# A hybrid decoder layer: products of the modulation rows in the first and in the second half of attention

## The chip, the cores and the metric

The kernel runs on one NeuronCore of a Trainium2 chip. A time is the microseconds (us) of the device from the start to the end of one execution; the runs of a kernel are compared by their median. A profile is one execution recorded by the hardware profiler. In profiles PE is TensorE's matmul, PEld its weight load, DVE the vector engine (VectorE), ACT ScalarE, POOL GpSimd, and SP the sequencer that issues most DMAs here.

## The reference

One decoder layer on x of 512 tokens by 2048, float32. What matters here is in three places:

```python
mod = silu(c) @ w_ada + b_ada                    # w_ada: 2048 x 12288
sh1, sc1, gt1, sh2, sc2, gt2 = split(mod, 6)     # six rows of 2048
h = rms_norm(x, g_pre_mix) * (1 + sc1) + sh1
proj = h @ w_in       # q, k/v of three branches, gates, RG-LRU branches
o_att = nsa_attention(...)   # 16 heads; compressed, selected and window branch
hr = rg_lru(causal_conv(xr)) # 8 channel blocks
mix = concat(rms_norm(o_att), rms_norm(gelu(yr) * hr)) @ w_out
x = x + gt1 * rms_norm(mix, g_post_mix)
h = rms_norm(x, g_pre_mlp) * (1 + sc2) + sh2
x = x + gt2 * rms_norm(square(relu(h @ w_ff1)) @ w_ff2, g_post_mlp)
```

The rows gt1, sh2 and sc2 (numbers 2, 3 and 4 in the kernel) are needed after attention: gt1 when the output projection is evacuated, sc2 and sh2 when the input of the MLP is formed. gt2 (number 5) is needed at the very end.

## The kernel before, in words

A matrix product in float32 is made of three matmuls in a rounded type (`mm3`, L176): every operand is split into a rounded part by ScalarE (L102 for weights) and a rest by VectorE (L103). Weights come by DMAs of 512 KB on the SP queue into two raw tiles (`wr`, L84).

Stages in order: the modulation rows 0 and 1 and the first projections; attention of head groups 0 and 1 (`attention(0, n1)`, L996), a changeover that forms keys and values of groups 2 and 3 (L997 to L1000), attention of groups 2 and 3 (`attention(1, ...)`, L1001); then the output projection (L1018 to L1186) and the MLP. Below, the two calls are the first and the second half of attention.

A half has 64 units, one for each head, branch (selected, window) and chunk of 128 queries. A unit has scores on TensorE, a masked minimum with the branch's key count on VectorE (`soft1`, L736), an exponential on ScalarE (L738), a reciprocal and a product with the gate on VectorE (L746, L747), a scaling on ScalarE (L748), transposes on TensorE (L755), and the split of the transposed rows on both (L766, L767). `sm` is a small tile of a unit's statistics, in a ring of six. The loop of `attention` (L958) has 70 steps, each working on several units at different points of this chain. Between them `fill` takes pieces of other work from a list: projections of later heads and the RG-LRU branch.

A modulation row that is not needed early is computed as products on VectorE (`qdot`, L208). Row s is cut into 64 pieces (16 blocks of 128 outputs, 4 stretches of 512 inputs). A piece loads a tile `md` of 128x512 of `w_ada` by a DMA on SP (256 KB, L217), multiplies it by the same stretch of silu(c), which stands in a tile `ca` on all partitions, and sums along the row (L218: one three-operand instruction and the read of its accumulator). `md` has four buffers in attention; `ca` has one and is loaded anew (L216) after every 16 pieces. Each step of the loop adds MRATE = 0.8 to a counter, and as often as it holds a whole one a piece is issued: rows 2, then 4, then 3. Whatever of rows 3 and 4 is left goes into the output projection (`cdots`, L1121), evenly over 36 places. The 64 pieces of row 5 run in the MLP.

The order on each engine is not the order of this code. A scheduler orders the instructions of all engines by priority (the place in the code) and by when they can run according to its own model; each engine then runs its list strictly in that order. A piece depends only on a free `md` buffer, its load and `ca`, so the scheduler can place it ahead of its place in the code.

Of the kernel before, what the change touches and what calls it, by code (L numbers as in the profile page):

```python
# [7 lines left out]
F32 = mybir.dt.float32  # L8
F32R = mybir.dt.float32r
AF = mybir.ActivationFunctionType  # L10
OP = mybir.AluOpType
# [16 lines left out]
Q_REST, K_REST, XR_T, YR_T = 0, 6, 8, 16  # L28


NA1, NA2, NMS, NTMP, NXI, NPC, NSB, TD, MRATE, NMD, NRT = 4, 10, 22, 6, 4, 2, 11, 3, 0.8, 4, 6
JOIN = [2, 1, 1, 1] * 5 + [2, 1, 1, 0, 3]
HALF, CA_ = 512, 1
PX = 0
# [96 lines left out]
def hybrid_block_kernel(ctx: ExitStack, tc: tile.TileContext, xT, c, vec, wada, wst, win, wv0, wv1,  # L131
                        w1, w2, pe, wrg, wout, wff1, wff2, xN, out):
    nc = tc.nc
    V, A, T, G = nc.vector, nc.scalar, nc.tensor, nc.gpsimd
# [68 lines left out]
    QD = {s_: [(k, q_) for q_ in range(4) for k in range(KT)] for s_ in (2, 3, 4, 5)}  # L203
    dq = {s_: const.tile([128, 4, KT], F32, name=f"dq{s_}") for s_ in QD}
    CA = {}
    cad = dram.tile([1, D], F32, name="cad")

    def qdot(pool, s_, n, ring=("md", NMD)):  # L208
        for _ in range(min(n, len(QD[s_]))):
            k, q_ = QD[s_].pop(0)  # L210
            w = pool.tile([128, S], F32, name="md", tag=ring[0], bufs=ring[1])
            if k == 0 or CA["pool"] is not pool:
                CA["pool"] = pool
                ca = CA[0] = pool.tile([128, S], F32, name="ca", tag="ca", bufs=1)
                row = cad[0, S * q_:S * q_ + S]
                nc.sync.dma_start(ca, bass.AP(tensor=row.tensor, offset=row.offset, ap=[[0, 128], [1, S]]))  # L216
            nc.sync.dma_start(w, wada[s_, k, :, S * q_:S * q_ + S])  # L217
            (V.scalar_tensor_tensor(w, w, 0.5, CA[0], op0=OP.mult, op1=OP.mult,  # L218
                                                            accum_out=dq[s_][:, q_, k:k + 1]))

    def qvec(o, s_, base=None, plus=0.0):
# [35 lines left out]
    def fill(n):  # L257
        for _ in range(n):
            if stream:
                stream.pop(0)()  # L260
# [389 lines left out]
    bp = bst.enter_context(tc.tile_pool(name="bp", bufs=1))  # L650
# [21 lines left out]
    def quad(pair, ep):  # L672
        return [((2 * pair + i % 2), 2 * ep + i // 2) for i in range(4)]
# [24 lines left out]
    def cmp_a2(pair, ep):  # L698
        p_, d_ = PC[pair, ep]
        pf = p_.rearrange("p c e n -> p (c e) n")  # L700
        V.reduce_sum(d_, pf, axis=AX.X)
        V.reciprocal(d_, d_)
        for i, (g, e_) in enumerate(quad(pair, ep)):
            dv = d_.rearrange("p (c e) -> p c e", c=4)[:, :, i]
            V.tensor_mul(dv, dv, gates[:, :, 3 * (4 * g + e_)])
        V.tensor_mul(pf, pf, d_[:, :, None].to_broadcast([128, 16, 32]))
# [12 lines left out]
    UN, HB = {}, {}  # L719

    def scores(u):
        h, br, ch = u
        n = 128 * (ch + 1)
        sp_ = ps("S")
        q_ = Q[h][:, 128 * ch:128 * ch + 128]
        T.matmul(sp_[:, :n], q_, KD[h // 4][:, br, 0, :n], start=True, stop=False)
        T.matmul(sp_[:, :n], q_, KD[h // 4][:, br, 1, :n], start=False, stop=True)
        UN[u] = [sp_]

    def soft1(u):  # L730
        h, br, ch = u
        n = 128 * (ch + 1)
        sp_ = UN[u][0]
        p_ = bp.tile([128, S], F32, name="pp", tag="pp", bufs=TD + 1)
        sm = bp.tile([128, 4], F32, name="sm", tag="sm", bufs=6)
        V.tensor_tensor_reduce(p_[:, :n], sp_[:, :n], mask[:, S - n:], scale=-0.125, scalar=3e38,  # L736
                               op0=OP.add, op1=OP.min, accum_out=sm[:, 0:1])
        A.activation(p_[:, :n], p_[:, :n], AF.Exp, bias=sm[:, 0:1], scale=-1.0, accum_out=sm[:, 1:2])  # L738
        UN[u] = [p_, sm]

    def soft2(u):
        h, br, ch = u
        n = 128 * (ch + 1)
        p_, sm = UN[u]
        gi = h * 3 + 1 + br
        V.reciprocal(sm[:, 2:3], sm[:, 1:2])  # L746
        V.tensor_mul(sm[:, 3:4], sm[:, 2:3], gates[:, ch, gi:gi + 1])  # L747
        A.activation(p_[:, :n], p_[:, :n], AF.Copy, scale=sm[:, 3:4])  # L748

    def trans(u):  # L750
        h, br, ch = u
        p_ = UN[u][0]
        pt = ps("T")
        for j in range(ch + 1):
            T.transpose(pt[:, 128 * j:128 * j + 128], p_[:, 128 * j:128 * j + 128], ident)  # L755
        UN[u] = [pt]

    def evac_t(u):
        h, br, ch = u
        n = 128 * (ch + 1)  # L760
        if ch == 0:
            HB[h, br] = [bp.tile([128, 13, 128], F32R, name=n_, bufs=1) for n_ in ("pth", "ptl")]
        th, tl = HB[h, br]
        pv_ = UN.pop(u)[0][:, :n].rearrange("p (j q) -> p j q", q=128)
        sl = slice(ch, 3 * ch + ch + 1, 3)
        A.activation(th[:, sl], pv_, AF.Copy)  # L766
        V.tensor_sub(tl[:, sl], pv_, f(th[:, sl]))  # L767
# [174 lines left out]
        add(lambda k=k: pre_out(k))  # L942
    n3 = len(stream)

    nmod = [0.0]

    def attention(pair, natoms):
        seq, info = [], {}
        for ep in range(2):
            for i, (g, e_) in enumerate(quad(pair, ep)):  # L950
                for br in range(2):
                    for ch in range(4):
                        u = (4 * g + e_, br, ch)
                        info[u] = (ep, i, 4 * pair + e_)
                        seq.append(u)
        n = len(seq)
        goal, done = len(stream) - natoms, 0
        for s_ in range(-1, n + TD + 2):  # L958
            def get(k):
                return seq[k] if 0 <= k < n else None  # L960
            if get(s_ - 1):
                soft2(get(s_ - 1))
            if get(s_ - TD - 1):
                evac_t(get(s_ - TD - 1))
            if get(s_):
                soft1(get(s_))
            if 0 <= s_ < n and s_ % 32 == CA_:
                cmp_a(pair, s_ // 32)
            if get(s_ + 1):
                scores(get(s_ + 1))  # L970
            tot = natoms * (s_ + 2) // (n + TD + 3)
            k = tot - done
            fill(k // 2)
            if get(s_ - TD):
                trans(get(s_ - TD))
            fill(k - k // 2)
            done = tot
            if 0 <= s_ < n:
                if s_ % 32 == CA_ + 1:
                    cmp_a2(pair, s_ // 32)  # L980
                if s_ % 32 == CA_ + 2:
                    cmp_b(pair, s_ // 32)
            u = get(s_ - TD - 1)
            if u and u[2] == 3:
                ep, i, t = info[u]
                pv(u[0], u[1], i, PC[pair, ep])
                if u[1] == 1:
                    head_out(u[0], i, t)
            nmod[0] += MRATE
            while nmod[0] >= 1:  # L990
                qdot(bp, 2 if QD[2] else 4 if QD[4] else 3, 1)
                nmod[0] -= 1
        fill(natoms - done)

# [196 lines left out]
    for g in range(4):  # L1191
        for q in range(NA1):
# [3 lines left out]
            for r in range(4):  # L1196
                half, j = r // 2, 2 * g + r % 2
# [350 lines left out]
    for s, (kind, q, g) in enumerate(GR):  # L1548
        if kind == "f":
            k, n = q  # L1550
# [110 lines left out]
    for n_, key in enumerate(XTODO):  # L1661
        n, j, half = key
        for c_ in range(2):
            y = Y[key][:, 256 * c_:256 * c_ + 256]
            V.scalar_tensor_tensor(y, y, rs[:, 2 * j + c_:2 * j + c_ + 1], XT[key][:, 256 * c_:256 * c_ + 256],
                                   op0=OP.mult, op1=OP.add)
# [68 lines left out]
```

## Time and profile before

| | |
|---|---|
| median of 3 runs | 2198.32 us (2195.87 to 2200.69) |
| profiled execution, whole | 2199.99 us |
| its span, first to last instruction | 2198.3 us |
| mean granted TensorE clock | 0.982 |
| busy: TensorE, VectorE, ScalarE | 2093.1, 1879.1, 1392.2 us |
| pieces (L218) | 256 |

How to read it: the busy share is of an engine's time between the start and the end of its instructions; matmuls overlap, so TensorE can look busier than it is. An idle stretch in front of an instruction is put down to what ended it. The granted clock is 1.0 at TensorE's 2.4 GHz and 0.5 at 1.2 GHz.

### The profile page before, as it was taken

How to read it: one execution, taken by the hardware profiler on the slowest of the kernel's cores; microseconds unless marked ns; L12 is line 12 of the kernel's file. 1: busy time of each engine (PE TensorE's matmuls, PEld its weight loads, DVE VectorE, ACT ScalarE, POOL GpSimd, SP SyncE). 2: the span in 40 equal slices, each digit the busy share in tenths (PEclk: the TensorE clock that was granted, in tenths of full speed). 3: DMA queues.
4: the chain of work that ended last, by engine and by line, in shares of the span. 5: the costliest groups of instructions: out<-in, count | busy, mean ns of one | idle time of the engine just before them, and what ended most of it. 6: DMA issues, size and time to landing. Idle time of an engine off the chain costs nothing.

```text
span 2198.3 us, 39410 instructions
## 1 busy us (share of the span) xinstructions
PE 2093.1 (95%) x14621; PEld 1911.7 (87%) x14621; DVE 1879.1 (85%) x3764; ACT 1392.2 (63%) x2536; POOL 63.5 (3%) x119
## 2 busy tenths in 40 slices
PE   7998999989999989999999999998999999999995
PEld 3686777778877867899999999998999999999995
DVE  8987989877887677889999999999888887887788
ACT  4349879648995226765555555545766777767764
POOL 0000000000000000000000000000000000000010
PEclk9999999999999999999999999999999999999998
DMA  9764544762127886555555555566766544544453
GB/s 380 309 234 139 189 158 149 219 199 68 59 85 225 275 290 203 180 191 175 184 180 171 175 186 178 194 206 207 248 218 217 188 164 141 165 151 157 138 171 116
DMA packets 138818, 411.12 MB, mean 187 GB/s; under 512 B 18225, under 2 KB 25281, under 8 KB 134273
## 3 DMA queue, kind: packets, MB, share of 16 engines
q1 hardware_dynamic: 126178, 341.49, 46.6%
q0 software_dynamic: 12448, 67.12, 8.8%
q8 instruction: 115, 1.88, 0.4%
q14 instruction: 77, 0.63, 0.1%
HBM read 366.58 MB, written 41.97 MB: 186 GB/s over the span
## 4 chain that ended last, share of the span: by engine, by line
PE 52%; issue 26%; DVE 12%; ACT 5%; DMA 5%; POOL 0%; SPq 0%; DVEq 0%; POOLq 0%; ACTq 0%
PE ps_pj L1132 3%; PE ps_pj L1133 3%; PE ps_pj L1134 3%; DMA md<-wada 3%; DVE fl L1300 3%; PE ps_pj L1479 2%; PE ps_pj L1480 2%; PE ps_pj L1481 2%; PE ps_T L1132 2%; PE ps_T L1134 2%; PE ps_T L1133 2%; PE ps_S L1134 2%; PE ps_S L1132 2%; PE ps_S L1133 2%; PE ps_S L1479 2%
## 5 line engine op out<-in xcount | busy, mean ns | idle before, releaser
L1299 ACT ACTIVATE fh<-fs 128x1024 fp32r<-128x1024 f32 x256 | 272.9, 1066 | 324.7 <-DVE fs L1318 139.6
L1300 DVE TENSOR_TENSOR fl<-fs,fh 128x1024 fp32r<-128x1024 f32 x256 | 312.3, 1220 | 98.2 <-ACT fh L1299 95.7
L1299 ACT ACTIVATE fh<-fr 128x768 fp32r<-128x768 f32 (+2 forms) x296 | 217.1, 735 | 67.5 <-PE ps_pj L1133 13.3
L1300 DVE TENSOR_TENSOR fl<-fr,fh 128x768 fp32r<-128x768 f32 (+2 forms) x296 | 239.9, 814 | 11.3 <-ACT fh L1299 11.3
L102 ACT ACTIVATE sl<-wr 128x512 fp32r<-128x512 f32 (+2 forms) x252 | 145.6, 606 | 150.7 <-DMA wr<-wout 93.4
L218 DVE SCALAR_TENSOR_TENSOR md<-md,ca 128x512 f32<-128x512 f32 x256 | 171.4, 685 | 62.8 <-DMA md<-wada 39.7
L103 DVE TENSOR_TENSOR sl<-wr,sl 128x512 fp32r<-128x512 f32 (+2 forms) x252 | 163.6, 662 | 47.8 <-ACT sl L102 32.7
L1315 DVE TENSOR_TENSOR fs<-fr 128x512 f32<-128x512 f32 x256 | 175.2, 684 | 5.8 <-DMA fr<-wff 4.1
L1479 PE MATMUL ps_pj<-fh,AH 128*128 128x256 f32 x602 | 169.1, 281 | 1.1 <-ACT ps_pj L1459 1.0
L1480 PE MATMUL ps_pj<-fl,AH 128*128 128x256 f32 x602 | 169.1, 281 | 0.0
L1481 PE MATMUL ps_pj<-fh,AL 128*128 128x256 f32 x602 | 168.8, 281 | 0.0
L177 PE MATMUL ps_pj<-AH,sl 128*128 128x512 f32 x384 | 161.7, 421 | 0.1
L179 PE MATMUL ps_pj<-AH,sl 128*128 128x512 f32 x384 | 153.1, 399 | 0.7 <-DVE sl L103 0.7
L178 PE MATMUL ps_pj<-AL,sl 128*128 128x512 f32 x384 | 153.2, 399 | 0.0
L1479 PEld LDWEIGHTS ps_pj<-fh,AH 128*128 128x128 f32 x602 | 113.9, 189 | 2.1 <-ACT ps_pj L1459 2.1
L1480 PEld LDWEIGHTS ps_pj<-fl,AH 128*128 128x128 f32 x602 | 114.0, 189 | 0.4 <-DVE fl L1300 0.4
L1481 PEld LDWEIGHTS ps_pj<-fh,AL 128*128 128x128 f32 x602 | 114.0, 189 | 0.0
L1480 PE MATMUL ps_S<-fl,AH 128*128 128x256 f32 x394 | 110.4, 280 | 2.8 <-DVE fl L1300 2.8
L1479 PE MATMUL ps_S<-fh,AH 128*128 128x256 f32 x394 | 110.5, 280 | 1.3 <-ACT ps_S L1459 1.2
L1318 DVE TENSOR_TENSOR fs<-fs,fr 128x256 f32<-128x256 f32 x256 | 107.6, 420 | 3.5
L1481 PE MATMUL ps_T<-fh,AL 128*128 128x256 f32 x396 | 110.6, 279 | 0.0
L1479 PE MATMUL ps_T<-fh,AH 128*128 128x256 f32 x396 | 110.6, 279 | 0.0
(633 smaller groups left out, 7283.8 us busy)
## 6 DMA issues: line engine op xcount, KB each, us to landing
fr<-wff SPq DMA_DIRECT2D x276, 512.0 KB, 3.7
md<-wada SPq DMA_DIRECT2D x256, 256.0 KB, 4.3
uf<-ud POOLq DMA_DIRECT2D x32, 896.0 KB, 4.9
wr<-win SPq DMA_DIRECT2D x48, 512.0 KB, 3.7
ada<-wada SPq DMA_DIRECT2D x22, 1024.0 KB, 10.2
wr<-wout SPq DMA_DIRECT2D x36, 512.0 KB, 4.9
ud<-uf POOLq DMA_DIRECT2D x18, 896.0 KB, 5.2
ud<-uf POOLq DMA_DIRECT2D x14, 768.0 KB, 4.9
```

The lines of the kernel that those rows point to most:

```text
L103: self.nc.vector.tensor_sub(lo, raw, self.f(hi))
L177: T.matmul(o, wh, mh, start=start, stop=False)
L218: (V.scalar_tensor_tensor(w, w, 0.5, CA[0], op0=OP.mult, op1=OP.mult, accum_out=dq[s_][:, q_, k:k + 1]))
L1132: T.matmul(o, wh, b[0], start=start, stop=False, skip_group_check=True)
L1133: T.matmul(o, wh, b[1], start=False, stop=False, skip_group_check=True)
L1134: T.matmul(o, wl, b[0], start=False, stop=stop, skip_group_check=True)
L1299: A.activation(hi, src, AF.Copy)
L1300: V.tensor_sub(lo, src, f(hi))
L1315: V.tensor_add(v2(Sm[:, :512]), v2(R[:, 256:768]), R[:, None, :256].to_broadcast([128, 2, 256]))
L1479: T.matmul(o, uh, hi, start=first and k < 4 and t_ == 0, stop=False, skip_group_check=True)
L1480: T.matmul(o, uh, lo, start=False, stop=False, skip_group_check=True)
L1481: T.matmul(o, ul, hi, start=False, stop=last, skip_group_check=True)
```

## The change

The rate of pieces becomes 0.4 per step in the first half and 1.7 in the second. In the second half every fourth piece (while the step has a unit) no longer takes its factor 0.5 as a constant but from a fifth column of the unit's `sm`, which a memset fills with 0.5 just before. So this piece can't be placed ahead of the tile `sm` of its step.

```diff
-NA1, ..., TD, MRATE, NMD, NRT = 4, 10, 22, 6, 4, 2, 11, 3, 0.8, 4, 6
+NA1, ..., TD, MR, NMD, NRT = 4, 10, 22, 6, 4, 2, 11, 3, (0.4, 1.7), 4, 6
...
-    def qdot(pool, s_, n, ring=("md", NMD)):
+    def qdot(pool, s_, n, ring=("md", NMD), half=0.5):
...
-            (V.scalar_tensor_tensor(w, w, 0.5, CA[0], op0=OP.mult, op1=OP.mult,
+            (V.scalar_tensor_tensor(w, w, half, CA[0], op0=OP.mult, op1=OP.mult,
...
-        sm = bp.tile([128, 4], F32, name="sm", tag="sm", bufs=6)
+        sm = bp.tile([128, 5], F32, name="sm", tag="sm", bufs=6)
...
-    nmod = [0.0]
+    nmod, ndot = [0.0], [0]
...
-            nmod[0] += MRATE
+            nmod[0] += MR[pair]
             while nmod[0] >= 1:
-                qdot(bp, 2 if QD[2] else 4 if QD[4] else 3, 1)
+                half = 0.5
+                if pair and get(s_) and ndot[0] % 4 == 0:
+                    half = UN[get(s_)][1][:, 4:5]
+                    V.memset(half, 0.5)
+                qdot(bp, 2 if QD[2] else 4 if QD[4] else 3, 1, half=half)
+                ndot[0] += 1
                 nmod[0] -= 1
```

On VectorE in the second half, at its eighth and ninth unit, this stood before (pp and sm are a unit's probabilities and statistics, sl a weight's rest):

```order
L736 ISA pp_4921,sm_4922<-ps_S_4895,mask_1075 128x512
L736 ISA sm_4922 128x1
L767 TENSOR_TENSOR ptl_4833<-ps_T_4905,pth_4832 128x4x128
L746 RECIPROCAL sm_4922<-sm_4922 128x1
L747 TENSOR_TENSOR sm_4922<-sm_4922,gates_72 128x1
L736 ISA pp_4957,sm_4958<-ps_S_4925,mask_1075 128x128
L736 ISA sm_4958 128x1
L103 TENSOR_TENSOR sl_5070<-wr_4853,sl_5069 128x512
L746 RECIPROCAL sm_4958<-sm_4958 128x1
L747 TENSOR_TENSOR sm_4958<-sm_4958,gates_72 128x1
```

And at the same two units this stands now (md and ca are a piece's operands, dq2 its result, L994 the memset):

```order
L736 ISA pp_4859,sm_4860<-ps_S_4829,mask_1075 128x512
L736 ISA sm_4860 128x1
L736 ISA pp_4898,sm_4899<-ps_S_4863,mask_1075 128x128
L736 ISA sm_4899 128x1
L994 MEMSET sm_4932 128x1
L218 SCALAR_TENSOR_TENSOR md_4995,dq2_91<-md_4995,ca_4679 128x512
L746 RECIPROCAL sm_4860<-sm_4860 128x1
L218 SCALAR_TENSOR_TENSOR md_4966,dq2_91<-md_4966,sm_4932,ca_4679 128x512
L747 TENSOR_TENSOR sm_4860<-sm_4860,gates_72 128x1
L746 RECIPROCAL sm_4899<-sm_4899 128x1
L218 SCALAR_TENSOR_TENSOR md_4998,dq2_91<-md_4998,ca_4679 128x512
L747 TENSOR_TENSOR sm_4899<-sm_4899,gates_72 128x1
```

Three pieces, one of them tied to a unit's `sm`, have come between the unit's own instructions. Counted over the whole list, before the first, up to the 32nd, from the 32nd to the 64th, and between the 64th and the 65th mask-add (L736) stood 33, 39 and 40 pieces, and none between the 65th and the last; 80 after it, without row 5's. Now it is 33, 8, 0, 95, and 56 after the last.

On the SP queue this stood before from the end of the changeover into the second half (wr is a weight's raw tile):

```order
L217 DMA md<-wada 128x512 x6
L84 DMA wr<-win 128x1024
L217 DMA md<-wada 128x512 x3
...
L84 DMA wr<-win 128x1024 x3
L84 DMA wr<-wrg 128x256
L84 DMA wr<-win 128x1024 x2
...
L84 DMA wr<-win 128x1024 x6
```

And this stands now in the second half:

```order
L217 DMA md<-wada 128x512 x7
L84 DMA wr<-win 128x1024
L217 DMA md<-wada 128x512 x5
...
L217 DMA md<-wada 128x512 x4
L216 DMA ca<-cad 128x512
L217 DMA md<-wada 128x512
...
L84 DMA wr<-wrg 128x256
L217 DMA md<-wada 128x512 x3
```

The weight loads of the second half, which followed one another, now have the loads of pieces and of `ca` between them; in the changeover it is the other way round.

## Rows read from the trace of the kernel before

**Rows 1.** Page: span, and busy time, share and instructions of each engine

```profile
span 2198.3 us, 39410 instructions
...
PE 2093.1 (95%) x14621; PEld 1911.7 (87%) x14621; DVE 1879.1 (85%) x3764; ACT 1392.2 (63%) x2536; POOL 63.5 (3%) x119
```

**Rows 2.** Busy time by stretch; columns in the first line

```profile
core 0: us, PE busy (x) PEld busy (x) DVE busy (x) ACT busy (x) POOL busy (x), PEclk, DMA share, GB/s
215.00:314.00 99.00, 95.04 (x485) 77.24 (x485) 91.99 (x300) 84.11 (x202) 1.78 (x3) 1.00 0.55 177
314.00:417.00 103.00, 97.67 (x499) 78.25 (x498) 96.54 (x317) 82.79 (x195) 2.16 (x4) 1.00 0.55 168
417.00:482.00 65.00, 59.84 (x369) 52.72 (x367) 47.63 (x126) 26.22 (x53) 0.54 (x1) 0.98 0.73 239
482.00:653.00 171.00, 165.43 (x851) 134.74 (x851) 141.38 (x444) 153.01 (x362) 3.24 (x6) 0.99 0.21 66
653.00:700.00 47.00, 44.15 (x186) 34.62 (x187) 39.14 (x69) 29.19 (x56) 1.08 (x2) 0.89 0.66 207
700.00:840.00 140.00, 130.69 (x542) 102.21 (x541) 96.33 (x240) 40.84 (x89) 0.00 (x0) 0.96 0.83 276
...
340.00:380.00 40.00, 39.33 (x199) 31.52 (x198) 39.44 (x124) 38.44 (x91) 1.08 (x2) 1.00 0.48 152
```

**Rows 3.** Line L736 within 482 to 653: count, ns min/median/max, first and last start

```profile
L736 DVE CUSTOM_DVE_ANT_0 pp<-ps_S,mask x64: 266/477/692, 482.3 to 651.9; 128x128 f32<-128x128 f32 x16, 128x256 f32<-128x256 f32 x16, 128x384 f32<-128x384 f32 x16, 128x512 f32<-128x512 f32 x16
```

**Rows 4.** Busy time of L218 by stretch; two records make a piece

```profile
core 0: us, DVE busy (x), PEclk, DMA share, GB/s
215.00:314.00 99.00, 22.51 (x66) 1.00 0.55 177
314.00:417.00 103.00, 26.43 (x78) 1.00 0.55 168
417.00:482.00 65.00, 26.78 (x80) 0.98 0.73 239
482.00:653.00 171.00, 0.00 (x0) 0.99 0.21 66
653.00:700.00 47.00, 0.00 (x0) 0.89 0.66 207
700.00:840.00 140.00, 52.84 (x160) 0.96 0.83 276
```

**Rows 5.** Timeline of VectorE: start us, duration us, instruction

```profile
439.93 0.67 DVE L218 SCALAR_TENSOR_TENSOR md<-md,ca 128x512 f32<-128x512 f32 x1
440.54 0.07 DVE L218 DVE_READ_ACCUMULATOR md<-md,ca 128x1 f32 x1
440.54 0.68 DVE L218 SCALAR_TENSOR_TENSOR md<-md,ca 128x512 f32<-128x512 f32 x1
...
441.15 0.68 DVE L218 SCALAR_TENSOR_TENSOR md<-md,ca 128x512 f32<-128x512 f32 x1
```

**Rows 6.** Instructions of VectorE by line, 200 to 440: busy us, mean ns | idle before

```profile
L218 DVE SCALAR_TENSOR_TENSOR md<-md,ca 128x512 f32<-128x512 f32 x87 | 58.5, 681 | 12.4 <-DMA md<-wada 5.8 <-DMA ca<-cad 4.5 <-issue 2.1
...
L805 DVE SCALAR_TENSOR_TENSOR xc<-xp,vecs,xc 128x512 f32<-128x512 f32 x12 | 9.0, 746 | 0.0
...
L800 DVE MEMSET xp<- 128x3 f32 x5 | 0.3, 61 | 0.0
```

**Rows 7.** What L218 waited for within 215 to 482: us, times

```profile
  DMA md<-wada: 13.3, 12
  DMA ca<-cad: 8.7, 3
```

**Rows 8.** Changeover: waits (us, times, longest), and timeline rows of ScalarE and TensorE

```profile
ACT sl L102 <- DMA wr<-win: 14.7, 5, 5.3
...
475.15 0.63 ACT L102 ACTIVATE sl<-wr 128x512 fp32r<-128x512 f32 x1 [5.27 <-DMA wr<-win]
...
481.13 1.24 PE L685 MATMUL ps_pj<-kc,qd 128*128 128x64 f32 x5 [3.95 <-DVE qd L253]
```

**Rows 9.** Projection: timeline rows of SP, ScalarE and TensorE

```profile
802.89 0.33 SPq L216 DMA_DIRECT2D ca<-cad  x1
803.27 1.39 SPq L217 DMA_DIRECT2D md<-wada  x2
804.76 0.38 SPq L84 DMA_DIRECT2D wr<-wout  x1
...
811.48 1.15 ACT L102 ACTIVATE sl<-wr 128x512 fp32r<-128x512 f32 x2 [6.89 <-DMA wr<-wout]
...
807.08 0.39 PE L917 MATMUL ps_pj<-sl,AL 128*128 128x512 f32 x1
812.16 0.80 PE L915 MATMUL ps_pj<-sl,AH 128*128 128x512 f32 x1 [4.69 <-ACT sl L102]
...
817.72 0.80 PE L916 MATMUL ps_pj<-sl,AH 128*128 128x512 f32 x1 [3.18 <-DVE sl L103]
```

More of the change, by code (lines that the diff above doesn't have):

```diff
@@ L28 @@
 Q_REST, K_REST, XR_T, YR_T = 0, 6, 8, 16
-NA1, NA2, NMS, NTMP, NXI, NPC, NSB, TD, MRATE, NMD, NRT = 4, 10, 22, 6, 4, 2, 11, 3, 0.8, 4, 6
+NA1, NA2, NMS, NTMP, NXI, NPC, NSB, TD, MR, NMD, NRT = 4, 10, 22, 6, 4, 2, 11, 3, (0.4, 1.7), 4, 6
 JOIN = [2, 1, 1, 1] * 5 + [2, 1, 1, 0, 3]
```

## Prediction

> **What bounds the kernel now.** The page comes first: over the whole span TensorE is busy 95% and the Vector engine 85% [rows 1]. That is an average over stages, so the second view is the table of stretches, cut where the change cuts [rows 2]. 215 to 314 and 314 to 417 us hold the 32 + 32 softmax units of the first half of attention. 417 to 482 is the changeover, 482 to 653 the 64 units of the second half (its first and last mask-add start at 482.3 and 651.9 [rows 3]); then come its tail with the start of the output projection, and the projection up to 840.
>
> In that table the Vector engine is the busiest but for TensorE in the first half (92.0 of 99 us, 96.5 of 103) and has room in the second (141.4 of 171). TensorE's busy time overlaps itself and says little. ScalarE is busy 84 and 83 us in the two early stretches and 153 of 171, that is 89%, in the second half.
>
> The third view is the same table for line L218 alone, the pieces of the modulation rows, each with its accumulator read, so two records a piece [rows 4]. There are 33 pieces before 314, 39 up to 417, 40 in the changeover, none from 482 to 700, and 80 in the projection. So 112 were written for attention, 56 a half, yet all were done before the second half began: the scheduler had pulled them forward. This is what the reader should see: the half that the change loads has no piece at all now, and 29.6 us of idle Vector time.
>
> **The change part by part.**
>
> *Counts.* 70 steps at 0.4 give 28 pieces, at 1.7 some 118 (the last fraction is lost), 146 in all against 112. The rest of the 192 pieces of rows 2, 4 and 3 falls from 80 to 46. In the order on VectorE the counts are 33, 8, 0, 95, 10 and 46 where they were 33, 39, 40, 0, 0 and 80. A piece that is tied to a step keeps one of the four buffers, so at most a few loose ones can get ahead: the hold works.
>
> *Cost of one piece.* Three pieces in a row start 0.61 us apart, though each is shown with 0.68 us and a read of 0.07 [rows 5]: an instruction overlaps the end of the one before. I take 0.61 us. The 27 tied ones add a one-column fill of 0.061 us [rows 6]. Their factor is a column in place of a constant: a three-operand instruction with a column takes 0.746 us against 0.681 with a constant [rows 6], so 0.065 us more. Together 27 x 0.126 = 3.4 us.
>
> *Second half, 482 to 653: loss.* The Vector engine has 141.4 us of work there; 95 x 0.61 = 58.0 and 3.4 make 202.8 in 171. Since it works in order, 31.8 us is the least that this stretch grows, with no idle time left at all. The other end adds waits at the head of its queue. The vector ca is reloaded every 16 pieces into one buffer, and pieces waited 8.7 us in 3 reloads and 13.3 us for their own rows among 112 [rows 7]: six reloads at 2.9 and 95 pieces at 0.12 are 28.8 us, so 60.6 in all. The nearest rows are the early stretches, where this engine is the bound with pieces among the units: 92.9% and 93.7% busy [rows 2], and 98.6% in their densest part, 340 to 380 [rows 2]. I take 95%, since ScalarE would then be busy only 153 of 213: 202.8 / 0.95 = 213.5, a loss of 42.5 us.
>
> *Tail, 653 to 700: loss.* 10 pieces of 0.61 are 6.1 us beside 39.1 of 47 busy [rows 2]. They fit the 7.9 us of idle time, but stand ahead of the normalization that TensorE needs next: between 0 and 6.1, taken as 2.
>
> *First half from 314 on: gain.* 31 pieces leave, 18.9 us of Vector work, the most that can be won; the least is nothing, if TensorE (97.7 of 103 busy) is the real limit. Without them Vector has 77.6 us and ScalarE's 82.8 is the largest next to TensorE. At the 89% that ScalarE reaches in the second half this stretch would take 92.5, a gain of 10.5. I take 8, nearer to the TensorE row.
>
> *Changeover: gain.* All 40 pieces leave. Vector was no bound here (47.6 of 65 busy), so their own 24 us are worth nothing. But their loads share the SP queue with the weights: ScalarE waited 14.7 us for weights, 5.27 of it at 475, and TensorE then stood 3.95 us [rows 8]. TensorE's idle time here is 5.2 us and the lower clock (0.98) accounts for 1.3 [rows 2]: between 0 and 6.5, taken as 4.
>
> *Projection, 700 to 840: gain.* The same pattern. At 802.9 the reload of ca and two rows are issued ahead of a weight, ScalarE waits 6.89 us for it, TensorE stands 4.69 and then 3.18 us at 812 and 817 [rows 9], and the granted clock over the stretch is 0.96, where it was 1.00 from 215 to 417 [rows 2]. Its idle time is 9.3 us, the clock at most 4% of 140 = 5.6: between 0 and 14.9. 34 of 80 pieces leave; that share of 14.9 is 6.3, and I take 7.
>
> *Sum.* 42.5 + 2 - 8 - 4 - 7 = +25.5 us. The profiled execution took 2199.99 us, 1.7 us around its span; 2225.5. It lies 1.7 us above the median of the runs, 2198.32, so about 2224 is forecast.
>
> **The rivals.**
>
> *The relief outweighs the load (faster).* Where Vector bounds the first half, what leaves it shortens the time one to one, and the freed SP queue lets TensorE run without standing. With every relieved stretch at its end, 18.9 + 6.5 + 14.9 = 40.3, and the second half at its floor of 31.8 with the tail free, the kernel would take 2199.99 - 8.5 - 1.7 = 2190. It decides from the point where the second half grows by less than the relief gives. For it: Vector at 94% in the first half. Against it: the floor is a count that nothing shortens, and TensorE is already close to continuous in the relieved stretches. The Trainium skill (Perfetto Trace Analysis, Optimization Strategy) says that where the most-contended engine changes between regimes, interleaving them may help. That rule speaks for this rival. The trace agrees that the bound changes (Vector 94% in the first half, ScalarE 89% in the second), but the second half has 29.6 us of idle Vector time for 61.4 us of new work, so evening out turns into overloading.
>
> *Weights of the second half come late (slower still).* In the new order on SP four to seven loads of pieces stand between two weight loads of the second half, where weights stood alone. A row cannot be issued until the piece four or so before it has run, and the weight behind it waits. The measured price is 14.7 us of weight wait for 40 pieces in the changeover [rows 8], of which TensorE lost 5.2; at 95 pieces 12 us, and with a fall of the clock as at 812 (a matmul there takes 0.80 us instead of 0.39 [rows 9]) up to 20: 2236 to 2244. For it: the same pattern stalls the projection. Against it: TensorE has slack once Vector bounds the half, and DMA is busy only 21% there against 83% in the projection [rows 2]. The skill (DMA: Bandwidth & Descriptors, Anatomy of one DMA) states that a semaphore wait is held by the issuing sequencer before dispatch, the DMA engines do not wait. That is the blocking meant here, and the issue times around 802.9 agree.
>
> *The hold fails* and the pieces run ahead as before: then only 34 pieces would move out of the projection, between 2184 and 2200. The order excludes it, and I give it 1%.
>
> **How the numbers follow.** This kernel's measurements can tell about 0.2%, 4.4 us, from no change. Forecast (Vector bounds the second half, relief gives back less than half): 68%, own range 2208 to 2238, from the floor with middling relief up to 52 us of loss with the relief as taken. Late weights: 17%. Relief about equal to the load or above it: 14%, spread from 2190 to 2207; the failing hold: 1%. Of these 15, 8 are faster by over 0.2% (below 2193.9) and 7 within 0.2%, with 1 more from the forecast's low end. Slower: 84%. The range is 2203 to 2246: it leaves one in ten at the low end and one in ten above, where the second half's waits reach their upper end with little relief.
>
> **What would show it.** In the profile after, the 64 units of the second half should span about 212 us instead of 170 with the Vector engine busy over 93% and ScalarE down to some 72%; 95 pieces lie in that stretch. The 32 units before should take about 95 us instead of 103, and the changeover about 61. In the projection TensorE's idle time should fall from 9.3 to a few us. I am wrong in the main step if the second half grows by under 32 us (then a piece costs less than 0.61 us beside other work), wrong in its size if Vector is idle over 10% there, and wrong in the relief if the stretch from 314 shortens by over 15 us or not at all.

## The result and the profile after

The changed kernel takes 2226.12 us (median of 4 runs, 2222.99 to 2229.05) where the kernel before takes 2197.46 beside it: a ratio of 1.0124, 95% interval 1.0109 to 1.014 (estimated from the single runs; the quotient of the two medians is 1.0130). Slower was forecast, at 2224 us. The profiled execution took 2224.39 us, 24.4 more than that of before.

The page of the changed kernel, its span and busy times, against [rows 1]:

```profile
span 2222.7 us, 39427 instructions
...
PE 2106.4 (95%) x14621; PEld 1922.0 (86%) x14621; DVE 1876.8 (84%) x3791; ACT 1398.9 (63%) x2538; POOL 63.7 (3%) x119
```

The Vector engine has done the same work (1876.8 us, 1879.1 before): nothing is added but 27 small fills, the time comes from the place. The table of stretches, cut at about the same events as [rows 2]; the last two lines split the second half at its 33rd unit (columns in the first line):

```profile
core 0: us, PE busy (x) PEld busy (x) DVE busy (x) ACT busy (x) POOL busy (x), PEclk, DMA share, GB/s
217.00:314.50 97.50, 94.38 (x483) 76.96 (x483) 91.84 (x300) 83.66 (x201) 1.79 (x3) 1.00 0.55 179
314.50:412.30 97.80, 93.56 (x485) 76.01 (x484) 80.47 (x250) 83.22 (x195) 2.17 (x4) 1.00 0.29 93
412.30:470.20 57.90, 57.90 (x357) 51.39 (x357) 24.11 (x47) 27.02 (x53) 0.54 (x1) 1.00 0.30 95
470.20:689.00 218.80, 186.88 (x886) 145.62 (x884) 197.10 (x666) 159.84 (x370) 3.79 (x7) 0.93 0.53 171
689.00:736.00 47.00, 42.00 (x169) 33.49 (x169) 40.94 (x88) 26.15 (x46) 0.54 (x1) 0.83 0.69 233
736.00:866.00 130.00, 130.00 (x559) 104.41 (x558) 77.33 (x175) 42.91 (x93) 0.00 (x0) 1.00 0.71 234
470.20:571.50 101.30, 93.34 (x485) 75.30 (x483) 92.86 (x319) 78.64 (x185) 1.09 (x2) 1.00 0.50 162
571.50:688.10 116.60, 92.64 (x397) 69.41 (x397) 103.34 (x345) 80.66 (x186) 2.71 (x5) 0.87 0.55 180
```

The reader is to see three things. The second half (470 to 689) now spans 218.8 us instead of 171, and VectorE is busy 197.1 of it, 90%. Units 33 to 64, in front of the changeover, span 97.8 with VectorE no longer near its limit (80.5). The changeover and the projection from 736 on have a TensorE that is busy without a gap at a clock of 1.00, where [rows 2] show idle time and 0.98 and 0.96. The pieces in the second half alone, two records each, as in [rows 4]:

```profile
470.20:689.00 218.80, 65.74 (x191) 0.93 0.53 171
```

The mask-adds of the second half, as in [rows 3], show its length, 470.2 to 688.1:

```profile
L736 DVE CUSTOM_DVE_ANT_0 pp<-ps_S,mask x64: 275/479/685, 470.2 to 688.1; 128x128 f32<-128x128 f32 x16, 128x256 f32<-128x256 f32 x16, 128x384 f32<-128x384 f32 x16, 128x512 f32<-128x512 f32 x16
```

What was waited for in the second half of the changed kernel (us, times, longest):

```profile
ACT pp L748 <- DVE sm L747: 19.1, 19, 2.8
...
DVE md L218 <- DMA ca<-cad: 7.4, 5, 2.7
...
PE ps_T L755 <- DVE ptl L767: 5.8, 4, 2.2
...
DVE md L218 <- DMA md<-wada: 3.9, 5, 1.7
...
ACT sl L102 <- DMA wr<-wout: 1.2, 1, 1.2
...
ACT sl L102 <- DMA wr<-wrg: 0.9, 1, 0.9
```

Of the waits of TensorE, VectorE and ScalarE, ScalarE's for VectorE's scale of a unit (L747) is the largest (GpSimd, busy 3% of the span, has longer ones), and VectorE itself stands 11.3 us for the operands of its pieces, 7.4 of them for the reload of ca. Weights make ScalarE wait 2.1 us in all. One such reload in the timeline of the changed kernel (start us, duration, instruction, in brackets the idle time before it and what ended it):

```profile
603.29 0.33 SPq L216 DMA_DIRECT2D ca<-cad  x1
603.66 0.42 SPq L217 DMA_DIRECT2D md<-wada  x1
...
605.01 0.68 DVE L103 TENSOR_TENSOR sl<-wr,sl 128x512 fp32r<-128x512 f32 x1
605.22 0.19 ACT L738 ACTIVATION_READ_ACCUMULATOR pp<-pp,sm 128x1 f32 x1
607.18 0.75 DVE L218 SCALAR_TENSOR_TENSOR md<-md,sm,ca 128x512 f32<-128x512 f32 x1 [1.49 <-DMA ca<-cad]
607.86 0.08 DVE L218 DVE_READ_ACCUMULATOR md<-md,sm,ca 128x1 f32 x1
607.86 0.69 DVE L218 SCALAR_TENSOR_TENSOR md<-md,ca 128x512 f32<-128x512 f32 x1
...
608.47 0.69 DVE L218 SCALAR_TENSOR_TENSOR md<-md,ca 128x512 f32<-128x512 f32 x1
...
609.08 0.16 DVE L746 RECIPROCAL sm<-sm 128x1 f32<-128x1 f32 x1
...
609.76 0.15 DVE L747 TENSOR_TENSOR sm<-sm,gates 128x1 f32<-128x1 f32 x1
...
610.00 0.40 ACT L748 ACTIVATE pp<-pp,sm 128x128 f32<-128x128 f32 x1 [2.96 <-DVE sm L746]
```

The reload is issued at 603.29 and VectorE reaches the piece that needs it when L103 ends. It stands 1.49 us, then runs the pieces that have gathered. The reciprocal of a waiting unit comes behind them, at 609.08, though the sum that it reads was there when ScalarE's read at 605.22 had ended, and ScalarE has idled 2.96 us for it. A short wait at the head of VectorE's list becomes a longer one on another engine.

For all kernels below, stage lengths are taken between starts of mask-adds (1st, 33rd, 64th, 65th, 128th) and up to the start of the last matmul of the projection (us, one profiled execution each; pieces that start in each stage behind):

| kernel | median | first 32 | units 33 to 64 | changeover | second half | tail and projection | pieces |
|---|---|---|---|---|---|---|---|
| before | 2197.46 | 98.4 | 102.8 | 65.4 | 169.5 | 213.6 | 33/39/40/0/80 |
| after | 2226.12 | 97.3 | 97.8 | 57.8 | 217.9 | 201.1 | 33/8/0/95/56 |
| e1_no_hold | 2190.96 | 98.7 | 101.8 | 70.0 | 172.4 | 199.4 | 33/38/45/30/46 |
| e2_hold_only | 2192.19 | 98.2 | 98.1 | 56.9 | 173.9 | 214.0 | 33/29/1/45/84 |
| e3_narrow | 2191.27 | 96.4 | 97.2 | 57.8 | 187.5 | 205.2 | 38/3/0/95/56 |
| e4_no_loads | 2210.47 | 95.5 | 96.0 | 57.8 | 209.7 | 200.6 | 32/0/0/104/56 |
| e5_mid | 2209.87 | 97.3 | 97.5 | 57.8 | 191.6 | 212.7 | 33/8/0/63/88 |
| e6_late_hold | 2206.22 | 96.0 | 103.1 | 64.7 | 189.1 | 200.9 | 33/39/39/41/40 |
| e7_changeover | 2191.84 | 99.3 | 97.4 | 67.6 | 179.4 | 200.5 | 33/23/38/44/54 |
| e8_changeover_free | 2187.58 | 97.2 | 102.3 | 56.8 | 181.2 | 199.0 | 33/39/22/44/54 |
| e9_one_ca | 2207.27 | 94.8 | 98.0 | 57.8 | 204.8 | 203.4 | 34/7/0/95/56 |
| e10_shared_ca | 2219.05 | 97.9 | 97.7 | 57.8 | 213.2 | 204.2 | 33/8/0/95/56 |
| e11_best_shared_ca | 2186.42 | 96.8 | 103.4 | 56.7 | 175.8 | 201.4 | 33/39/22/45/53 |

The first 32 units, which hold 32 to 38 pieces in every kernel, scatter from 94.8 to 99.3: a difference of some 2 us in one stage of one execution is not told apart. The profiled execution can also lie several us from the median of its kernel: 4.9 above it in e6_late_hold (2211.09), 4.2 below it in e11_best_shared_ca (2182.18).

### The profile page after: what moved, and what is told of

Same layout as the page of the kernel before. It is cut to its first block, busy times and chain, and to the rows that moved or that the text cites. A ratio compares the mean times of both kernels' runs of the same rounds, so it can differ in the third digit from the quotient of the medians.

```text
span 2222.7 us, 39427 instructions
## 1 busy us (share of the span) xinstructions
PE 2106.4 (95%) x14621; PEld 1922.0 (86%) x14621; DVE 1876.8 (84%) x3791; ACT 1398.9 (63%) x2538; POOL 63.7 (3%) x119
## 4 chain that ended last, share of the span: by engine, by line
PE 65%; DVE 17%; DMA 8%; ACT 6%; issue 3%; SPq 0%; DVEq 0%; ACTq 0%; POOLq 0%
PE ps_pj L1137 3%; PE ps_pj L1139 3%; DMA md<-wada 3%; PE ps_pj L1138 3%; PE ps_pj L1484 3%; PE ps_pj L1485 3%; DVE md L218 3%; PE ps_pj L1486 3%; DVE fl L1305 2%; PE ps_T L1139 2%; PE ps_T L1137 2%; PE ps_T L1138 2%; PE ps_S L1139 2%; PE ps_S L1137 2%; PE ps_S L1138 2%
## 5 line engine op out<-in xcount | busy, mean ns | idle before, releaser
L1305 DVE TENSOR_TENSOR fl<-fr,fh 128x768 fp32r<-128x768 f32 (+2 forms) x296 | 239.8, 814 | 12.4 <-ACT fh L1304 12.3
L103 DVE TENSOR_TENSOR sl<-wr,sl 128x512 fp32r<-128x512 f32 (+2 forms) x252 | 163.1, 663 | 72.7 <-ACT sl L102 36.2
L218 DVE SCALAR_TENSOR_TENSOR md<-md,ca 128x512 f32<-128x512 f32 x229 | 153.3, 685 | 50.7 <-DMA md<-wada 28.7
L1485 PE MATMUL ps_T<-fl,AH 128*128 128x256 f32 x396 | 110.8, 280 | 0.0
```

The source lines that it names most:

```text
L103: self.nc.vector.tensor_sub(lo, raw, self.f(hi))
L218: (V.scalar_tensor_tensor(w, w, half, CA[0], op0=OP.mult, op1=OP.mult, accum_out=dq[s_][:, q_, k:k + 1]))
L1305: V.tensor_sub(lo, src, f(hi))
L1485: T.matmul(o, uh, lo, start=False, stop=False, skip_group_check=True)
```

## The experiments

The theory: the pieces put more work on VectorE in the second half than its idle time holds, and the half grows by the excess. The rivals: it is the loads (weights late, or VectorE standing for rows), or the tie.

**The new rates without the tie.** The pieces may run ahead again.

```diff
-                if pair and get(s_) and ndot[0] % 4 == 0:
-                    half = UN[get(s_)][1][:, 4:5]
-                    V.memset(half, 0.5)
```

> The rates of the change (0.4 and 1.7) without the tie: every piece takes its factor as a constant. In the order 30 of the pieces then stand in the second half (95 in the change), 45 in the changeover, 46 in the projection. Occupancy theory (the second half grows by VectorE's added work once its idle time is used): 141.4 + 30 x 0.61 = 160 us of VectorE work fit the 171 us, so the second half grows by 0 to 4 us, the projection keeps its relief of about 10 us, and the kernel takes 2188 to 2195. Queue theory (weight loads come late behind loads of pieces): about 4 us more in the second half, 2192 to 2198. Tie theory (memset, column factor and the held sm tiles cost the time): the whole loss goes, 2185 to 2195. E1 alone does not part the first from the third; E2 does.

Measured: 0.9975 of before (0.9964 to 0.9986). Without the tie 30 pieces stay in the second half, which grows by 2.9 us, the changeover loses 4.6 and the projection, with 34 pieces fewer, gains 14.2. The rates alone are a gain of 0.25%; the loss comes with the tie or with what it keeps in the second half. All three theories allow this result; the next runs part them.

**The tie with the old rates.**

```diff
-..., MR, NMD, NRT = ..., (0.4, 1.7), 4, 6
+..., MR, NMD, NRT = ..., (0.8, 0.8), 4, 6
```

> The tie without the new rates (0.8 in both halves): 45 pieces in the second half, 1 in the changeover, 62 in the first half, 84 after. Occupancy theory: 141.4 + 45 x 0.61 + 1.5 = 170.4 us of VectorE work, at 90 to 95% busy 180 to 189 us in place of 171; relief of the changeover 7 us and of the first half 2; no relief in the projection: 2197 to 2208. Queue theory: half the pieces of the change, so about half of its 48 us in the second half: +24, less 9: 2210 to 2215. Tie theory: 14 ties of 27, about +24 too.

Measured: 0.9978 (0.9968 to 0.9987), faster than the 2197 to 2208 that I had expected. The second half grows by 4.4 us with 45 pieces, 12 of them tied, where the tie and the queue theory asked for about 24. The 32 units before the changeover, and the second half in two parts of 32 units:

```profile
314.10:412.20 98.10, 95.25 (x489) 76.85 (x489) 90.55 (x293) 82.14 (x194) 2.16 (x4) 1.00 0.47 152
...
469.00:557.40 88.40, 86.08 (x446) 69.60 (x445) 80.64 (x272) 75.15 (x177) 1.08 (x2) 1.00 0.38 121
557.40:642.90 85.50, 81.63 (x430) 65.60 (x429) 82.75 (x273) 77.31 (x184) 2.16 (x4) 1.00 0.44 145
```

The same two parts in the kernel before:

```profile
482.30:567.30 85.00, 82.84 (x417) 67.61 (x417) 67.88 (x214) 73.53 (x173) 1.08 (x2) 0.97 0.21 66
567.30:651.90 84.60, 82.29 (x434) 66.83 (x432) 72.26 (x229) 78.38 (x188) 2.16 (x4) 1.00 0.20 66
```

In before, VectorE has 17.1 and 12.3 us to spare. With 45 pieces it is busy 82.75 of 85.5 us in the second part, 97%, and the part is 0.9 us longer; the first grows by 3.4. Here work that fits the idle time costs little.

**Pieces of 32 columns.** The loads, the tie and the count stay, only L218 is short.

```diff
-            (V.scalar_tensor_tensor(w, w, half, CA[0], ...
+            (V.scalar_tensor_tensor(w[:, :nc_], w[:, :nc_], half, CA[0][:, :nc_], ...
...
-                qdot(bp, ..., 1, half=half)
+                qdot(bp, ..., 1, half=half, nc_=32 if pair else S)
```

> The change, but every piece that the second half issues multiplies and sums 32 of its 512 columns; its load, its buffer, its tie and its place stay (95 in the second half). The rest of these 118 sums is left out. Occupancy theory: a piece of 32 columns takes 0.15 to 0.2 us, so 141.4 + 95 x 0.18 + 3.4 = 162 us of VectorE work in the second half: it grows by 0 to 8 us in place of 48, the kernel takes 2176 to 2190. Queue theory: the loads stay, and with them most of the loss: 2210 to 2226. Tie theory: the ties stay, 2210 to 2226.

Measured: 0.9974 (0.9965 to 0.9984). The second half, the untied pieces, and what VectorE waited for in front of L218 there:

```profile
467.30:656.00 188.70, 174.19 (x875) 138.98 (x873) 153.10 (x666) 152.87 (x361) 3.24 (x6) 0.97 0.60 195
...
L218 DVE SCALAR_TENSOR_TENSOR md<-md,ca x69: 171/188/194, 470.9 to 651.0; 128x32 f32<-128x32 f32 x69
...
its engine sat idle before it (us, times) until:
  DMA md<-wada: 17.3, 22
  DMA ca<-cad: 4.2, 3
```

A piece takes 0.19 us instead of 0.68, VectorE has 153 us of work, and the half is 30 us shorter than in the changed kernel. But it is still 18 us longer than before, where at most 8 had been expected, and VectorE waits 21.5 us at pieces, 17.3 of them for rows. The ties are still there as well, but these waits point to the loads: they can cost time too, where the pieces are so short that VectorE catches up with them.

**No loads of rows.** The pieces have their full length, and ca is still loaded, six times.

```diff
-            nc.sync.dma_start(w, wada[s_, k, :, S * q_:S * q_ + S])
+            if load:
+                nc.sync.dma_start(w, wada[s_, k, :, S * q_:S * q_ + S])
...
+                qdot(bp, ..., 1, half=half, load=not pair)
```

> The change, but the pieces that the second half issues load nothing: they multiply ca by itself, in full width, with ring, tie and place as they were (104 in the second half). The products of these 118 rows are left out. Occupancy theory: VectorE has 141.4 + 104 x 0.61 + 3.4 = 208 us of work there, some 4 us of waits for loads go: the second half still takes 212 to 225 us, the kernel 2210 to 2230. Queue theory: nothing stands between the weight loads any more, the second half returns to 175 to 190 and the kernel to 2180 to 2195.

Measured: 1.0063 (1.0046 to 1.0079). The second half:

```profile
464.70:675.00 210.30, 185.33 (x883) 145.25 (x882) 201.36 (x684) 159.93 (x370) 3.78 (x7) 0.93 0.20 63
```

VectorE is busy 201.4 of 210.3 us, 96%, with 104 pieces: without any load of a row the half is 40 of the 48 us longer, or about 35 if the 9 more pieces are taken off at 0.6 each. VectorE waits 2.4 us in all for the six reloads of ca here. The 35 and the 18 us of the run before it make more than 48. That part of the waits lies beside work would explain this; it is not shown.

**A middle rate.**

```diff
-..., MR, NMD, NRT = ..., (0.4, 1.7), 4, 6
+..., MR, NMD, NRT = ..., (0.4, 1.2), 4, 6
```

> The change with 1.2 in place of 1.7 in the second half: 63 pieces there (0, 30, 45 and 95 in the kernels before), 88 after it (112 to 120 attention pieces in all). If the second half is free up to VectorE's idle time and then pays a piece in full (0.61 us and the waits for its loads, 0.9 us from 45 to 95 pieces), 63 pieces make it 173.9 + 18 x 0.9 = 190 us; if every piece costs the same (48 us for 95), 169.5 + 63 x 0.51 = 202 us. With the relief of the changeover and the first half as in the change (7.5 and 5 us) and the projection as before, the kernel takes 2203 to 2210 by the first, 2215 to 2222 by the second.

Measured: 1.0058 (1.0044 to 1.0071). The second half:

```profile
469.10:662.00 192.90, 175.12 (x884) 140.36 (x882) 177.30 (x595) 156.90 (x369) 3.25 (x6) 0.97 0.45 147
```

63 pieces make it 22 us longer: 191.6 by the table, near the 190 of the first reading and not the 202 of the second. The projection, with 88 pieces, is as slow as in before (212.7).

**The tie from the 108th piece only, rates 0.8 and 1.5.**

```diff
-                if pair and get(s_) and ndot[0] % 4 == 0:
+                if pair and get(s_) and ndot[0] >= 108 and ndot[0] % 4 == 0:
```

> A version that should beat both kernels: 0.8 in the first half and 1.5 in the second, and the tie only from the 108th piece on, so that earlier ones still run ahead. In the order 72 pieces in the first half, 39 in the changeover, 41 in the second half, 40 after it. Occupancy theory: the second half has 141.4 + 41 x 0.61 + 1.5 = 168 us of VectorE work and grows by 3 to 6 us, the projection with its tail gets 14 to 16 us shorter as without the tie, the rest stays as before: 2186 to 2192. If the tie itself or the loads in the second half cost the time (0.51 us a piece from the first on), the second half grows by 21 us and the kernel takes 2200 to 2206.

Measured: 1.0037 (1.0024 to 1.005), and my expectation was wrong. 41 pieces cost 19.6 us here, close to the 21 of the rival (every piece costs the same from the first on), which for the 45 pieces of the run with the tie alone would ask for 23 where 4.4 were measured. So the count alone does not decide. The two parts of the second half:

```profile
480.60:565.50 84.90, 82.11 (x413) 66.97 (x414) 67.89 (x213) 73.64 (x173) 1.08 (x2) 0.98 0.19 65
565.50:669.70 104.20, 88.36 (x439) 68.66 (x437) 97.90 (x327) 85.13 (x198) 2.71 (x5) 0.95 0.50 163
```

All 41 pieces lie in the second part. The first is as in before; in the second VectorE has 97.9 us of work where the part lasted 84.6 before, and it takes 104.2, busy 94%. I had counted pieces over the whole half. By these two runs the work of each part against its length counts; room in the first part is lost.

**No reload of ca in the second half.**

```diff
-            if k == 0 or CA["pool"] is not pool:
+            if (k == 0 and reload) or CA["pool"] is not pool:
...
+                qdot(bp, ..., 1, half=half, reload=not pair)
```

> The changed kernel, but in the second half the vector ca is not loaded anew after 16 pieces; the pieces there multiply by the stretch that is left in it, so the sums of those rows are other sums. Row loads and instructions stay. Theory A (VectorE's waits at the head of its queue for ca are lost time): the second half shortens by 5 to 9 us, from 218 to 209 to 213, and the whole is 2217 to 2221. Theory B (the wait for ca only takes the place of other idle time, since rows behind it are late as well): waits for md rise by about the same, within 2 us of the changed kernel, 2224 to 2228.

Measured: 1.0044 (1.0028 to 1.006), 19 us below the changed kernel, more than either side expected. The second half in two parts:

```profile
466.30:562.30 96.00, 92.43 (x485) 75.54 (x483) 92.22 (x319) 77.58 (x182) 1.08 (x2) 1.00 0.50 163
562.30:671.10 108.80, 86.39 (x397) 63.08 (x396) 103.14 (x347) 81.43 (x188) 2.70 (x5) 0.95 0.56 184
```

VectorE has the same work as in the changed kernel (195.4 and 196.2 us), but the half is 13.1 us shorter, VectorE busy 95%. The other 6 us lie in other stages, within their scatter. That makes 2.2 us for each of six reloads, while VectorE's own wait for them was 7.4 us in all; the timeline above shows one way in which more can follow from it. The list of this kernel differs in places from the changed one's, so its waits and its new order are not fully apart; the next run keeps the rows' own ca.

**Half the reloads.** Rows 2 and 4 are taken in turn, 16 pieces each, and share a load of ca.

```diff
-            if k == 0 or CA["pool"] is not pool:
+            if CA["q"] != q_ or CA["pool"] is not pool:
...
+    def row_():
+        a, b = (len(QD[s_]) for s_ in (2, 4))
+        return 2 if a and (a + 15) // 16 >= (b + 15) // 16 else 4 if b else 3
```

> The changed kernel with rows 2 and 4 taken in turn, 16 pieces each, so that both use one load of ca; counts of pieces by stretch stay 33, 8, 0, 95, 56, and the reloads of ca in the second half fall from six to three. Theory (a reload of ca stops VectorE at the head of its queue and costs about 13/6 = 2.2 us each, by the run without reloads): the second half shortens by 5 to 8 us, the whole is 2217 to 2221. Rival (the run without reloads was fast for its changed schedule, not for its waits): within 2 us of the changed kernel, 2224 to 2228.

Measured: 1.0094 (1.008 to 1.0109), 2219.05 us, and the second half is 4.7 us shorter, just under the 5 to 8 expected: 1.6 us a reload. VectorE's waits in front of pieces in the second half (L218 is L222 in this kernel):

```profile
its engine sat idle before it (us, times) until:
  DMA md<-wada: 4.9, 7
  DMA ca<-cad: 3.7, 3
```

The wait for ca has halved, that for rows has grown by 1. The direction holds, but the size is rough: the interval just touches that of the changed kernel (from 1.0109), and 4.7 us is not far above the scatter of one stage. Nor is it the full VectorE alone that makes a reload dear. In the run without loads of rows VectorE is just as full, and there a reload lands 3.1 to 3.8 us after its issue, in the changed kernel 4.3 to 5.7, with 2.4 and 7.4 us of waits for the six. So 1.6 to 2.2 us is the price of a reload beside the loads of rows.

**Versions that use what is free.** The old rates with the tie, and 30 more pieces written into the changeover.

```diff
+    hk_ = bp.tile([128, 1], F32, name="hk", bufs=1)
+    V.tensor_scalar(hk_, f(KD[2][:, 0, 0, 0:1]), 0.0, 0.5, op0=OP.mult, op1=OP.add)
+    for i_ in range(30):
+        qdot(bp, 2 if QD[2] else 4 if QD[4] else 3, 1, half=hk_ if i_ < 4 else 0.5)
```

> Rates 0.8 in both halves, the tie kept in the second half, and 30 more pieces written at the end of the changeover, the first four tied to a column computed there. On VectorE the counts are 33, 23, 38 in the changeover, 44 in the second half, 118 after, row 5's included. Theory (the density of pieces within a unit's idle time decides): 44 even pieces cost the second half 4 to 5 us as in the run with the hold alone, the changeover takes back its 65 us, the 32 units before it gain 2 to 4, the projection with 16 pieces fewer than in the hold-alone run gains 8 to 11 us over before. Whole: 2184 to 2190 us, 0.994 to 0.997 of before. Rival (pieces in the changeover cost what they cost before, and the projection gives nothing more under 56 pieces): 2192 to 2196.

Measured: 2191.84 us, 0.997 (0.9959 to 0.9981), above the expected 2184 to 2190 and at the lower end of the rival's 2192 to 2196: the pieces in the changeover did cost there what they cost before. Units 33 to 64, then the changeover:

```profile
316.00:413.30 97.30, 94.36 (x486) 76.16 (x485) 87.67 (x280) 83.06 (x195) 2.17 (x4) 1.00 0.43 137
413.30:480.90 67.60, 63.65 (x384) 55.89 (x383) 48.58 (x128) 26.50 (x53) 0.54 (x1) 0.98 0.69 227
```

38 pieces in the changeover cost 10 us there against the 57 to 58 of an empty one. The second half grew by 9.9 where 4 to 5 was expected. The next one is without the tie in the changeover (`i_ < 0`), so 16 of them run earlier:

> The same as the run before it but with no tie on the 30 pieces of the changeover, so they are free to run ahead into the first half: 33, 39, 22, 44, 118 pieces. Theory: the 32 units before the changeover are VectorE-bound again and take 102 to 103 us instead of 99, the changeover gains 2 to 4 for its 16 pieces fewer; whole 2186 to 2193, at most 3 us from the tied one. Rival (first half not bound by VectorE at 39 pieces): 2 to 4 us faster than the tied one.

Measured: 2187.58 us, 0.9956 (0.9941 to 0.9971), faster than both kernels. The two intervals overlap, so that it is faster than the one above is not shown, though the medians lie 4.3 us apart where I had expected at most 3. Units 33 to 64, changeover, second half:

```profile
314.20:416.50 102.30, 97.09 (x490) 78.01 (x489) 96.40 (x317) 82.77 (x195) 2.17 (x4) 0.98 0.52 169
416.50:473.20 56.70, 56.70 (x353) 50.40 (x352) 36.81 (x92) 26.28 (x53) 0.54 (x1) 1.00 0.64 207
473.20:655.00 181.80, 169.87 (x876) 135.98 (x874) 164.63 (x547) 154.37 (x365) 3.25 (x6) 1.00 0.39 128
```

The 22 pieces left in the changeover are free (56.7 us, clock 1.00): the gain there is 10.8 us, not the 2 to 4 expected. The 32 units before it are full again (96.4 of 102.3), as in before, so the rival's reason for a gain, that VectorE does not bind them, is not what made it. With ca shared as well:

> The version with 39, 22 and 45 pieces up to the changeover, in it and in the second half, and with ca shared by rows 2 and 4; reloads of ca fall from eight to about four up to the end of attention. Theory: a reload costs 1 to 2 us where VectorE bounds (the 32 units before the changeover and the second half), so 2183 to 2187. Rival (where pieces fit into idle time a reload costs nothing): 2187 to 2190, as without the sharing.

Measured: 2186.42 us, 0.9958 (0.9944 to 0.9971), not told apart from the run before it. Its second half:

```profile
473.00:650.00 177.00, 168.88 (x876) 135.69 (x874) 165.71 (x550) 155.00 (x367) 3.25 (x6) 1.00 0.41 132
```

So 44 or 45 pieces spread over the half cost 4.4, 9.9, 11.7 and 6.3 us in four kernels with 163 to 166 us of VectorE work each. The split by parts accounts for most of the difference. The second part in the two dear kernels, e7_changeover and e8_changeover_free:

```profile
570.20:660.30 90.10, 82.17 (x425) 65.24 (x425) 85.29 (x287) 78.42 (x187) 2.17 (x4) 1.00 0.44 143
...
563.80:654.40 90.60, 82.20 (x426) 65.21 (x425) 85.29 (x286) 78.47 (x187) 2.17 (x4) 1.00 0.44 142
```

26 of their 44 pieces lie there, and the 85.3 us of VectorE work are more than the 84.6 us that the part lasted before: it grows by 5.5 and 6.0. The two cheap kernels have 23 pieces and 82.8 and 83.8 us of work there, and it grows by 0.9 and 1.9. In the first part the four cost 3.4 to 5.6 us though VectorE is idle for 7.8 to 11.9 us of it; why stays open.

## Why the prediction was right

**Second half, forecast +42.5, measured +48.4.** The mechanism stands: the narrow pieces take away 30 us of it, the pieces without loads keep 35 to 40. The count of 95 pieces in the half was right too. Two parts of the sum were off, in opposite directions. The work added is 55.7 us (197.1 against 141.4) and not 61.4, so 0.59 us for a piece with its share of the tie. And the 95% busy that I divided by is reached where ca is not reloaded (195.4 of 204.8) or where no rows are loaded (201.4 of 210.3). With both loads it is 90%, and the half 13.1 us longer than without reloads. I had priced the reloads, at 2.9 each, but for the upper end only, and had taken a busy share a little above that of the early stretches, where pieces waited at 3 reloads in 267 us [rows 7]; here they waited at 5 in 219. So the sign of over 93% busy failed, and the idle share, 9.9%, is at the edge of what I had named as wrong in size. ScalarE at 73% is as forecast.

**Units 33 to 64, forecast -8, measured -5.0.** 23, 8, 3 and no pieces all end near 96 to 98 us, so that stretch has another limit, TensorE or ScalarE (which of them is not shown), some 5 us under the 103 of before. The caution about TensorE was right.

**Changeover, forecast -4, measured -7.6.** More than the upper end of 6.5. That end was made of idle time and clock for a fixed amount of TensorE work; the stretch now has 357 matmuls where [rows 2] has 369, so work has left it too. The runs show its shape: 0 to 22 pieces 57 to 58 us, 38 to 45 pieces 65 to 70.

**Tail and projection, forecast +2 and -7, measured -12.5 together.** The projection from 736 to 866 has no idle TensorE time at all, where 9.3 us were there in [rows 2]. ScalarE still waits for weights, 58.1 us against 87.6 by the waits of the two stretches, but TensorE no longer stands for it. Through all kernels, 40 to 56 pieces give 199 to 205 us and 80 to 88 give 213 to 214. TensorE's two stands in the middle of the projection (4.69 and 3.18 us in [rows 9]) recur in the two other kernels with 80 pieces and more, 3.73 and 3.56 with 84 and 4.92 and 3.18 with 88, and in none with 40 to 56. That is no share of 14.9 in proportion to the pieces, as I took it: with 34 pieces fewer nearly all of the harm is gone, and further ones bring little.

**The sum.** The terms made +25.5, the profiled executions differ by 24.4: the second half 6 us dearer, the relief 8 us larger (25.1 against 17), and the other stages 1 us. So the mechanism was right, but that the total came within 2 us of the measured one is luck: two misses of 6 and 8 us cancel. One bound does not follow from its own terms: 52 us of loss with the relief as taken is 52 + 2 - 19 = 35 us, or 2233, not the 2238 given as the upper end of the forecast's own range.

**The rivals.** Late weights: out. ScalarE's waits for weights in the second half come to 2.1 us where 12 were forecast, and in the run with pieces of 32 columns, whose loads are all there, to nothing. What the loads cost is paid in front of VectorE's pieces. The blocking I saw on the SP queue does exist there: loads of rows stand 88.3 us in the second half until a piece has run (L217 for L218). The Trainium skill (DMA: Bandwidth & Descriptors, Anatomy of one DMA), in a section on DMAs that GpSimd issues, puts such a wait on the issuing sequencer, and the trace agrees for SP. But the loss sits on the consuming engine's list: 1.49 us at 605.7, VectorE idle until the reload issued at 603.29 had landed. Relief outweighs: out for this change, since 95 pieces exceed the room by far. But its reasoning was sound for less of it: the Trainium skill's rule (Perfetto Trace Analysis, Optimization Strategy), that regimes with different bounds can be interleaved, agrees with the runs with 30 to 45 spread pieces, at 0.9956 to 0.9978 of before, and not with the 95 of this change. The hold fails: out, 95 pieces lie where the order put them; the run without the tie, at 2190.96, lies in the 2184 to 2200 that this rival gave.

The clock fell in the second part of the half (0.87, and 1.00 in the first), where TensorE is busy 92.6 of 116.6 us. I had not forecast it. With TensorE waiting for VectorE there, its own price can't be read from these runs.

## What to carry to other kernels

Before filler work is moved under a stage, count the idle time of its engine in pieces of that stage (here 32 units), and keep the work in each below the time that it lasted before. No amount was free over the whole half: 30 pieces cost 2.9 us (154.8 us of VectorE work in a half that lasted 169.5), 44 or 45 spread out 4 to 12 (163 to 166), 41 in one part 20, and 95 cost 48 (196). Count the reloads of shared operands with it, since VectorE stood at five of six here, and ScalarE, which waited for it, stood longer (1.49 and 2.96 us in the timeline); order the work so that a load serves more pieces. And look for the stretch that is hurt by what it holds now: relief can be had by moving only that part (22 of 40 pieces may stay in the changeover and 54 of 80 in the projection at next to no cost).

## What the runs showed that I had not expected

A tie on every fourth piece changed where the untied ones went, too: with the rates untouched, the pieces in the changeover fell from 40 to 1, and the kernel became 0.2% faster. A reload of one 128x512 tile costs roughly 1.6 to 2.2 us of the stage where VectorE is full and rows are loaded beside it, while its own idle time in front of the reloads shows 1.2 on average (7.4 over six).
